# Where the tiles of a one-core fp32 model step stand in on-chip memory: tiles moved within 512 bytes

## The chip, the cores and the metric

The kernel runs on one core of a Trainium2 chip. The metric is device time in microseconds (us) for one execution of the whole program; the median of three runs of the kernel before is 1243.19 us. TensorE (PE) does the matrix products, VectorE (DVE) and ScalarE (ACT) the element-wise work, GpSimd (POOL) a few masks, SyncE (SP) issues the transfers. SBUF is the on-chip memory with 128 partitions, in which all operands of a product lie; PSUM takes the products.

## What is computed

Two model blocks in a row on 256 tokens of width 1024, all in fp32. The first has a mixer of three branches, attention over a memory of 256 rows and a squared-ReLU MLP; the second has a state-space mixer, a gated convolutional FFN, latent attention and a second such FFN. Cut to the products that the change touches:

```python
def first_block(x, mem, ...):
    h = rmsnorm(x, norm_mix_g)
    proj = h @ w_in                       # three branches and gates
    ...                                   # conv, stick-breaking attention, retention
    up = jnp.einsum('bsnw,nwd->bsnd', branches, w_branch)
    x = x + jnp.sum(gates * up, axis=2) @ w_o
    x = x + memory_attention(rmsnorm(x, norm_xa_g), rmsnorm(mem, norm_mem_g), w_xq, w_xkv, w_xo)
    h = rmsnorm(x, norm_mlp_g)
    x = x + jnp.square(jax.nn.relu(h @ w_up)) @ w_down
    return rmsnorm(x, final_g)

def second_block(h, ...):
    h = layer_norm(ALPHA * h + ssd_mixer(h, ...))
    h = layer_norm(ALPHA * h + conv_ffn(h, ffn_up[0], ..., ffn_down[0]))
    h = layer_norm(ALPHA * h + mla_attention(h, ...))
    return layer_norm(ALPHA * h + conv_ffn(h, ffn_up[1], ..., ffn_down[1]))
```

## The kernel before

All weights, some 225 MB, pass through SBUF once. They are cut into chunks of at most 2048 elements per partition. A chunk arrives in `wr` (two buffers), ACT copies it to `wh` in the fp32r format that PE multiplies, DVE writes the remainder to `wl` (four buffers each). Activations are held the same way, as pairs of a high and a low part: `ah`/`al` (the input of a stage, made by `new_act`), `brh`/`brl` (branches), `mth`/`mtl` (merged), `memTh`/`memTl`, `oTh`/`oTl`, `gTh`/`gTl`, `yTh`/`yTl`, `cTh`/`cTl`. Each product is three matmuls (`mm3`): high by high, high by low, low by high.

A matmul has two operands in SBUF. One is loaded into the array 128 columns at a time (the profile's PEld rows, LDWEIGHTS), the other streams past it (the MATMUL rows). The kernel uses both directions:

- `wstat`: weights are loaded, the activation of 256 tokens streams past them. Output names stand as `mm<-ah,wh`: the operand ahead of the comma streams.
- `xstat`: the activation is loaded, weights stream past in blocks of up to 512 columns (`mm<-wh,ah`, 512 columns).
- `wmixed`: the first three chunks of three stages, activation loaded, 256 columns of weights streaming (`mm<-wh,ah`, 256 columns).

While one matmul streams, the LDWEIGHTS of the next one runs. Streaming matmuls run in unbroken rows of some twenty to nine hundred, between which stand transposes and the small products of the attention parts.

Places in SBUF follow from the order in which pools are opened and tiles are first asked for. `dynamic_dma_scratch_size` is a reserve at the lower end of SBUF, 16 KB per partition by default. What matters in this case is the place of a tile modulo 512 bytes; all steps inside the tiles named here (the next 128 columns, the next row of 256 tokens) are multiples of 512 bytes, except in the chunks of 320 and 384 columns of one stage (`kvq`) and in one chunk of 32 columns. A helper `gap` (L938 to L940) takes room in a pool without using it; before, it is called once, in `attention` with 704 bytes.

The order of the instructions comes from a planner (`Plan`, `tick`) that works with durations by kind and size; it knows nothing of addresses. Every engine operation is recorded at line L284, the helper's `call`.

Of the kernel before, what the change touches and what calls it, by code (L numbers as in the profile page):

```python
# [6 lines left out]
F32 = mybir.dt.float32  # L7
F32R = mybir.dt.float32r
# [8 lines left out]
P = 128  # L17
D = 1024
S = 256
ALPHA = 4 ** 0.25  # L20
NG = 8
RAW, HELD = 2, 4
# [198 lines left out]
class Slots:  # L221
    def __init__(self, kern, pool, name, shape, dtype, n):
        self.kern, self.at, self.pool, self.name, self.shape, self.dtype = kern, kern.at, pool, name, shape, dtype
        self.idle = list(range(n))
        self.out, self.old, self.lent = {}, {}, {}
# [237 lines left out]
        self.sync = Lane(plan, nc.sync, "sp")  # L463


class Kern:
    def __init__(self, nc, tc, a, dbg=None):
        self.at = Plan()
        self.nc, self.tc, self.a, self.dbg = Engines(nc, self.at), tc, a, dbg
        self.plan, _ = chunk_plan()  # L470
        self.nch = len(self.plan)
        self.n_dma = self.n_prep = self.n_half = self.n_get = self.n_done = 0
        self.raw, self.held, self.subs = {}, {}, []
        self.bg = []
        self.floor = 0.0
        self.turns = {}
        self.blocked, self.table = False, None
        self.work = self.skew = 0.0
        self.sums = np.concatenate([[0.0], np.cumsum([len(ks) * max(n, P) * UNIT for _, ks, _, n, _ in self.plan])])

# [336 lines left out]

    def new_act(self):

        return (self.acts.tile([P, 8, S], F32R, tag="ah", name="ah"), self.acts.tile([P, 8, S], F32R, tag="al", name="al"), [0, 0])  # L820

    def ready(self, act, k, *taus):
        if len(act) == 3:
# [113 lines left out]

    def gap(self, pool, n):  # L938

        pool.tile([P, n // 4], F32, tag="gap", name="gap")  # L940

    def pair(self, pool, name, n):
        return tuple(pool.tile([P, n, S], F32R, tag=name + x, name=name + x) for x in "hl")
# [12 lines left out]
    def mixers(self, act):  # L956
        nc, a = self.nc, self.a
        mp, mp_close = self.open("mix")
        br = self.pair(mp, "br", 12)
        gt = Slots(self, mp, "gt", [P, 3, S], F32, 4)  # L960
        r256 = Slots(self, mp, "r256", [P, 256], F32, 6)
# [261 lines left out]
        ap_close()  # L1223
        rp, rp_close = self.open("merged", side="right")
        mt = self.pair(rp, "mt", 8)
        memT = self.pair(rp, "memT", 8)
        gm = self.bcast("mem", self.gb, "gb")
        g_mem = self.spawn(self.mem_norm(gm, memT))
        for m in range(8):
# [27 lines left out]
    def memory(self, x, mt, memT, mt_close):  # L1257
        nc, a = self.nc, self.a
        act = self.new_act()
        ga = self.bcast("xa", self.gb, "gb")  # L1260
        mp, mp_close = self.open("mem")
        oT = self.pair(mp, "oT", 8)

        kT = (mp.tile([P, 8, S], F32R, tag="kT", name="kT"), mt[1])
        qs = Slots(self, mp, "qs", [P, 2, 2, S], F32R, 2)

        pTs = [tuple(k[:, 2 * h:2 * h + 2, :] for k in kT) for h in range(4)]
# [497 lines left out]
    def attention(self, h, act):  # L1765
        nc = self.nc
        cos, sin = self.cs[:, 0], self.cs[:, 1]
        pool, close = self.open("mla")
        self.gap(pool, 704)
        cT = self.pair(pool, "cT", 5)  # L1770
        krT = pool.tile([P, S], F32, tag="krT", name="krT")
        knT = pool.tile([P, 8, S], F32, tag="knT", name="knT")
        qnT = pool.tile([P, 8, S], F32, tag="qnT", name="qnT")
        qrT = pool.tile([P, 4, S], F32, tag="qrT", name="qrT")
        v = pool.tile([P, 2, D], F32, tag="v", name="v")
        oT = self.pair(pool, "oT", 8)
        ps_ = Slots(self, pool, "p", [P, 384], F32, 3)
        pT = Slots(self, pool, "pT", [P, 384], F32, 3)
# [189 lines left out]
    def program(self):  # L1968
        nc, tc, a = self.nc, self.tc, self.a
        cs = []  # L1970

        def pool(name, bufs=1, **kw):
            cm = tc.tile_pool(name=name, bufs=bufs, **kw)
            cs.append(cm)
            return cm.__enter__()

        cp = pool("const")
        self.gb = pool("gb", 2)  # L1980
        self.dram = pool("dram", space=bass.MemoryType.DRAM)
        self.acts = pool("acts")
        cq = pool("small")
        self.tiny = pool("tiny", 4)
        self.tk = Slots(self, pool("tk"), "tk", [P, D], F32, 2)
        self.wraw, self.whi, self.wlo = pool("wraw", RAW), pool("whi", HELD), pool("wlo", HELD)
        pp = pool("ps", space=PSUM)
        self.mm = Slots(self, pp, "mm", [P, 512], F32, 4)
        self.sm = Slots(self, pp, "sm", [P, 512], F32, 4)

        x = cp.tile([P, 2, D], F32, tag="x", name="x")
        self.cst = cst = cq.tile([P, NCST], F32, tag="cst", name="cst")
        self.ones = cp.tile([P, P], F32, tag="ones", name="ones")
        nc.vector.memset(self.ones, 1.0)

        row = self.tk.get()
        o, w = ROWS["mix"]
        nc.sync.dma_start(out=row[0:1, :], in_=a["prow"][0:1, o:o + w])
        halves = [slice(512 * n, 512 * n + 512) for n in range(2)]
        for c in halves:  # L2000
            nc.sync.dma_start(out=x[:, 0, c], in_=a["x"][0:P, c])
        nc.sync.dma_start(out=cst[:, 0:P], in_=a["cst"][:, 0:P])
        self.pump(1)
        nc.sync.dma_start(out=x[:, 1, :], in_=a["x"][P:2 * P, :])
        self.pump()
        nc.sync.dma_start(out=cst[:, P:], in_=a["cst"][:, P:])
        gs = [self.mm.get() for c in halves]
        for pt, c in zip(gs, halves):
            self.mm1(pt, self.ones[0:1, :], row[0:1, c], True)
        self.tk.put(row)  # L2010
        self.pcol = cp.tile([P, NCOL], F32, tag="pcol", name="pcol")
        nc.sync.dma_start(out=self.pcol, in_=a["pcol"])
        self.ident, self.nu, self.ut = (cst[:, CST[n]:CST[n] + P] for n in ("ident", "nu", "ut"))
        self.at.one = cq.tile([1, 2], F32, tag="one", name="one")
        nc.vector.memset(self.at.one, 1.0)
        self.neg1 = cp.tile([P, P], F32, tag="neg1", name="neg1")
        nc.vector.memset(self.neg1, -1.0)
        self.mhalf = cq.tile([P, 2], F32, tag="mhalf", name="mhalf")
        nc.vector.memset(self.mhalf, -0.5)
        self.identb = cp.tile([P, P], BF16, tag="identb", name="identb")  # L2020
        nc.vector.tensor_copy(self.identb, self.ident)

        self.maskb = cp.tile([P, P], BF16, tag="maskb", name="maskb")
        nc.vector.memset(self.maskb, 0.0)
        nc.gpsimd.affine_select(out=self.maskb, in_=self.maskb, compare_op=ALU.is_ge, fill=-1e30, base=0,
                                pattern=[[-1, P]], channel_multiplier=1)

        act = self.new_act()
        self.until(self.spawn(self.rms(0, x, Halves(gs), act), first=True))

        def second():
            yield from self.rms(1, x, Halves(gs), act)
            for pt in gs:
                self.mm.put(pt)

        self.spawn(second(), first=True)
        mt, memT, mt_close = self.mixers(act)
        self.spawn(self.angles(cp))
        act, close = self.memory(x, mt, memT, mt_close)
        act = self.mlp(x, act, close)  # L2040
        act = self.ssd(x, act)
        act = self.ffn(0, x, act)
        act = self.attention(x, act)
        self.ffn(1, x, act)
        self.drain()
        assert self.n_get == self.nch
        for cm in reversed(cs):
            cm.__exit__(None, None, None)
# [21 lines left out]
```

## Time and profile before

| | |
|---|---|
| three runs | 1238.36, 1243.19, 1243.27 us |
| profiled execution, its time | 1244.83 us |
| its span from first to last instruction | 1243.1 us |
| TensorE clock granted, mean | 0.998 of full speed |
| PE busy with matmuls | 1224.7 us, 8468 matmuls |
| DVE, ACT busy | 853.9 us, 717.0 us |

Outside the span lie 1.7 us. A matmul's row in the profile lasts from its issue to its last result, so rows of successive matmuls overlap; what a matmul costs in an unbroken row is the step, the time from the start of one to the start of the next. It is read from a stretch: the length of the stretch plus the duration of one matmul (0.28 us at 256 columns, 0.39 us at 512), divided by the number of matmuls that lie in it in whole or part.

### The profile page before, as it was taken

The page shows a single profiled execution, that of the slowest core. Times are in us where ns is not written, and L with a number is a line of the kernel's source. Part 1 is how long each engine was busy: PE and PEld are TensorE (multiplying, and loading weights), DVE is VectorE, ACT ScalarE, POOL GpSimd, SP SyncE. Part 2 cuts the span into 40 slices and gives each one's busy share as a digit, 9 for nine tenths or more (in the row PEclk, how much of TensorE's full clock was granted, in tenths as well). Part 3 has the DMA queues.
Part 4 walks back from the last instruction along what each step waited for, and adds up shares of the span by engine and source line. Part 5 has one row for each costly group of instructions (what it writes and reads, how often), then busy time and mean ns, then how long its engine had stood idle before and what let it go on. Part 6 is the DMA issues. An engine that isn't in the chain of part 4 may idle for free.

```text
span 1243.1 us, 20768 instructions
## 1 busy us (share of the span) xinstructions
PE 1224.7 (99%) x8468; PEld 1120.8 (90%) x8468; DVE 853.9 (69%) x1378; ACT 717.0 (58%) x1181; POOL 53.5 (4%) x85
## 2 busy tenths in 40 slices
PE   7999999999999999999999999999999999999997
PEld 5978999989989998889999898999988888999986
DVE  5666847666746665446787797877765866888853
ACT  5666546446536554335788765666644575666641
POOL 0011000000000000000111201000000000000000
PEclk9999999999999999999999999999999999999999
DMA  7643355546544546524656555555573443455560
GB/s 254 235 167 127 146 196 219 179 156 228 176 152 159 214 172 221 201 106 166 227 190 233 193 174 194 187 172 202 184 259 118 161 181 123 172 197 182 213 256 35
DMA packets 35425, 227.71 MB, mean 183 GB/s; under 512 B 4321, under 2 KB 4993, under 8 KB 11522
## 3 DMA queue, kind: packets, MB, share of 16 engines
q1 hardware_dynamic: 35330, 226.39, 50.8%
q8 instruction: 66, 1.08, 0.4%
q14 instruction: 29, 0.24, 0.1%
HBM read 225.27 MB, written 1.10 MB: 182 GB/s over the span
## 4 chain that ended last, share of the span: by engine, by line
PE 95%; DVE 3%; DMA 1%; issue 0%; ACT 0%; POOL 0%; SPq 0%; POOLq 0%; DVEq 0%; ACTq 0%
PE mm L284 85%; PE sm L284 9%; DVE wl L284 1%; DVE x L284 1%; DMA wr<-wts 0%; DVE tk L284 0%; DMA cst<-cst 0%; POOL rs L284 0%; ACT wh L284 0%; DVE ln L284 0%; DVE al L284 0%; SPq L284 0%; POOLq L2066 0%; ACT r L284 0%; ACT ah L284 0%
## 5 line engine op out<-in xcount | busy, mean ns | idle before, releaser
L284 DVE TENSOR_TENSOR wl<-wr,wh 128x1024 fp32r<-128x1024 f32 (+3 forms) x408 | 479.4, 1198 | 173.7 <-ACT wh L284 173.0
L284 ACT CAST wh<-wr 128x1024 fp32r<-128x1024 f32 (+3 forms) x408 | 403.6, 1029 | 162.4 <-PE mm L284 87.9
L284 PE MATMUL mm<-ah,wh 128*128 128x256 f32 (+1 forms) x1496 | 421.1, 281 | 0.0
L284 PE MATMUL mm<-ah,wl 128*128 128x256 f32 (+1 forms) x1496 | 417.5, 279 | 0.0
L284 PE MATMUL mm<-al,wh 128*128 128x256 f32 (+1 forms) x1496 | 417.4, 279 | 0.0
L284 PEld LDWEIGHTS mm<-ah,wh 128*128 128x128 f32 (+1 forms) x1496 | 283.0, 189 | 1.6 <-issue 1.1
L284 PEld LDWEIGHTS mm<-ah,wl 128*128 128x128 f32 (+1 forms) x1496 | 281.0, 188 | 0.1
L284 PEld LDWEIGHTS mm<-al,wh 128*128 128x128 f32 (+1 forms) x1496 | 280.5, 188 | 0.4
L284 DVE SCALAR_TENSOR_TENSOR r<-mm,pcol,r 128x255 f32<-128x255 f32 (+2 forms) x212 | 86.9, 474 | 38.6 <-ACT r L284 38.6
L284 PE MATMUL mm<-wl,ah 128*128 128x512 f32 (+3 forms) x320 | 106.3, 338 | 3.1 <-DVE wl L284 3.0
L284 PE MATMUL mm<-wh,ah 128*128 128x512 f32 (+3 forms) x320 | 108.6, 345 | 0.0
L284 PE MATMUL mm<-wh,al 128*128 128x512 f32 (+3 forms) x320 | 105.9, 337 | 0.5 <-DVE al L284 0.5
L284 PE MATMUL mm<-wh,gTh 128*128 128x512 f32 x304 | 96.3, 391 | 0.0
L284 PE MATMUL mm<-wh,gTl 128*128 128x512 f32 x304 | 95.6, 389 | 0.0
L284 PE MATMUL mm<-wl,gTh 128*128 128x512 f32 x304 | 95.6, 390 | 0.0
L284 ACT ACTIVATE r<-mm,pcol 128x256 f32<-128x256 f32 x96 | 48.9, 560 | 46.9 <-PE mm L284 46.9
L284 PEld LDWEIGHTS mm<-wl,ah 128*128 128x128 f32 x320 | 60.3, 189 | 10.2 <-DVE wl L284 4.9
L284 PEld LDWEIGHTS mm<-wh,gTl 128*128 128x128 f32 x304 | 57.1, 188 | 11.8
L284 PEld LDWEIGHTS mm<-wl,gTh 128*128 128x128 f32 x304 | 57.1, 188 | 11.8
L284 PEld LDWEIGHTS mm<-wh,gTh 128*128 128x128 f32 x304 | 56.7, 188 | 12.0 <-issue 0.6
L284 PEld LDWEIGHTS mm<-wh,al 128*128 128x128 f32 x320 | 60.3, 189 | 7.0 <-DVE al L284 1.1
L284 PEld LDWEIGHTS mm<-wh,ah 128*128 128x128 f32 x320 | 60.3, 189 | 6.6 <-issue 0.7
(296 smaller groups left out, 1581.8 us busy)
## 6 DMA issues: line engine op xcount, KB each, us to landing
wr<-wts SPq DMA_DIRECT2D x186, 1024.0 KB, 4.9
wr<-wts SPq DMA_DIRECT2D x11, 768.0 KB, 4.3
gb<-prow SPq DMA_DIRECT2D x12, 512.0 KB, 6.8
dec<-rows SPq DMA_DIRECT2D x8, 768.0 KB, 7.5
wr<-wts SPq DMA_DIRECT2D x4, 704.0 KB, 4.2
wr<-wts SPq DMA_DIRECT2D x4, 512.0 KB, 7.0
tk<-mem SPq DMA_DIRECT2D x2, 512.0 KB, 7.9
out<-x SPq DMA_DIRECT2D x4, 256.0 KB, 2.1
```

The lines of the kernel that those rows point to most:

```text
L284: r = f(*args, **kw)
```

## The change

No instruction is added, removed or moved on any engine, and one wait is added (below). What changes is where tiles stand. The scratch reserve shrinks from 16 KB to 1 KB per partition, and its room goes to gaps: 192 bytes ahead of the weight buffers, gaps of 320 and 192 bytes in several pools, and 512 bytes more in each half of `new_act`, whose tile is entered at an offset from the list `PLACES`, one entry for each of the seven stages that ask for one.

Places modulo 512, from the addresses in the two built programs:

| tile | before | after |
|---|---|---|
| `wr`, `wh`, `wl` | 288 | 480 |
| `ah`, `al` | 480 | 288 (480 in the sixth stage, latent attention) |
| `brh`, `brl` | 288 | 288 |
| `mth`, `mtl` | 480 | 480 |
| `memTh`, `memTl` | 480 | 288 |
| `oTh`, `oTl` of the memory attention, `gT`, `yT` | 288 | 480 |
| `cTh`, `cTl` | 480 | 288 |
| `oTh`, `oTl` of the latent attention | 480 | 480 |

Call **lag** the place of the tile that streams less the place of the tile that is being loaded meanwhile, modulo 512. Then:

| products | columns streaming | lag before | lag after |
|---|---|---|---|
| `wstat` on `ah`/`al`, `memT`, `cT` | 256 | 192 | 320 |
| `wstat` on `br` | 256 | 0 | 320 |
| `wmixed` on `ah`/`al` | 256 | 320 | 192 |
| `xstat` on `ah`/`al`, `memT`, `cT` | 512 | 320 | 192 |
| `xstat` on `mt`, and on `oT` of the latent attention | 512 | 320 | 0 |
| `xstat` on `gT`, `yT`, `oT` of the memory attention | 512 | 0 | 0 |

The added wait: the mask that POOL puts on the third `dec` buffer of the state-space mixer, which waited for the buffer's transfer, now also waits for ACT, which wrote `mth` in the same place in the branch merge of the first block.

The diff, cut to its core:

```diff
+PLACES = (320, 320, 320, 320, 320, 0, 320)
...
     def new_act(self):
 
-        return (self.acts.tile([P, 8, S], F32R, tag="ah", name="ah"), self.acts.tile([P, 8, S], F32R, tag="al", name="al"), [0, 0])
+        at = PLACES[self.n_act] // 4
+        self.n_act += 1
+        h, l = (self.acts.tile([P, 8 * S + 128], F32R, tag=n, name=n)[:, at:at + 8 * S].rearrange("p (k s) -> p k s", s=S) for n in ("ah", "al"))
+        return (h, l, [0, 0])
...
     def mixers(self, act):
         mp, mp_close = self.open("mix")
+        self.gap(mp, 320)
         br = self.pair(mp, "br", 12)
...
         mt = self.pair(rp, "mt", 8)
+        self.gap(rp, 320)
         memT = self.pair(rp, "memT", 8)
+        self.gap(rp, 192)
...
         oT = self.pair(mp, "oT", 8)
+        self.gap(mp, 320)
         kT = (mp.tile([P, 8, S], F32R, tag="kT", name="kT"), mt[1])
+        self.gap(mp, 192)
...
         pool, close = self.open("mla")
-        self.gap(pool, 704)
+        self.gap(pool, 320)
         cT = self.pair(pool, "cT", 5)
...
         v = pool.tile([P, 2, D], F32, tag="v", name="v")
+        self.gap(pool, 192)
         oT = self.pair(pool, "oT", 8)
...
-        self.wraw, self.whi, self.wlo = pool("wraw", RAW), pool("whi", HELD), pool("wlo", HELD)
+        self.gap(pool("gap0"), 192)
+        self.wraw, self.whi = pool("wraw", RAW), pool("whi", HELD)
+        self.wlo = pool("wlo", HELD)
...
-    nc = bacc.Bacc("TRN2", target_bir_lowering=False, num_devices=1)
+    nc = bacc.Bacc("TRN2", target_bir_lowering=False, num_devices=1, dynamic_dma_scratch_size=1024)
```

## Rows read from the trace of the kernel before

**Rows 1.** The page, busy time: engine, us (share of span), instructions.
```profile
PE 1224.7 (99%) x8468; PEld 1120.8 (90%) x8468; DVE 853.9 (69%) x1378; ACT 717.0 (58%) x1181; POOL 53.5 (4%) x85
```

**Rows 2.** The page, chain that ended last, shares by engine.
```profile
PE 95%; DVE 3%; DMA 1%; issue 0%; ACT 0%; POOL 0%; SPq 0%; POOLq 0%; DVEq 0%; ACTq 0%
```

**Rows 3.** PE groups by form: output<-streaming,loaded, columns, count | busy us, mean ns | idle.
```profile
L284 PE MATMUL mm<-ah,wh 128*128 128x256 f32 x1488 | 418.9, 281 | 0.0
...
L284 PE MATMUL mm<-wh,gTh 128*128 128x512 f32 x304 | 96.3, 391 | 0.0
...
L284 PE MATMUL mm<-wh,ah 128*128 128x512 f32 x144 | 59.0, 410 | 0.0
...
L284 PE MATMUL mm<-wh,ah 128*128 128x256 f32 x144 | 41.0, 285 | 0.0
...
L284 PE MATMUL mm<-brh,wh 128*128 128x256 f32 x96 | 27.3, 285 | 0.0
...
L284 PE MATMUL mm<-wh,oTh 128*128 128x512 f32 x64 | 21.9, 403 | 0.0
...
L284 PE MATMUL mm<-memTh,wh 128*128 128x256 f32 x64 | 17.8, 278 | 0.0
...
L284 PE MATMUL mm<-wh,memTh 128*128 128x512 f32 x32 | 12.8, 399 | 0.0
...
L284 PE MATMUL mm<-wh,mth 128*128 128x512 f32 x32 | 10.7, 396 | 0.0
```

**Rows 4.** Timeline, PE and weight loads: start us, us, engine, line, operation.
```profile
820.06 0.28 PE L284 MATMUL mm<-ah,wl 128*128 128x256 f32 x1
820.06 0.19 PEld L284 LDWEIGHTS mm<-ah,wh 128*128 128x128 f32 x1
```

**Rows 5.** Stretches, PE alone, `wstat`: from:to, length, busy us (matmuls), clock, DMA share, GB/s.
```profile
27.00:49.00 22.00, 22.00 (x190) 1.00 0.67 242
...
139.00:182.00 43.00, 43.00 (x382) 1.00 0.52 184
...
282.00:297.00 15.00, 15.00 (x135) 1.00 0.52 192
...
399.50:470.00 70.50, 70.50 (x601) 1.00 0.54 195
...
794.50:899.40 104.90, 104.90 (x893) 1.00 0.52 181
...
1073.70:1174.70 101.00, 101.00 (x893) 1.00 0.54 188
```

**Rows 6.** Stretches, PE alone: `br` product, `gT`, `mt`, and a `z` product on `ah`.
```profile
236.00:250.00 14.00, 14.00 (x119) 1.00 0.56 198
...
470.50:556.00 85.50, 85.50 (x379) 1.00 0.49 180
...
252.00:269.00 17.00, 17.00 (x76) 1.00 0.42 155
...
641.00:650.00 9.00, 9.00 (x40) 1.00 0.32 119
```

**Rows 7.** Timeline, PE, first and last of an unbroken `wmixed` stretch, second FFN.
```profile
1058.66 0.28 PE L284 MATMUL mm<-wh,al 128*128 128x256 f32 x1
...
1064.90 0.28 PE L284 MATMUL mm<-wl,ah 128*128 128x256 f32 x1
```

**Rows 8.** Timeline, PE, first and last of an unbroken `wmixed` stretch, first FFN.
```profile
780.17 0.28 PE L284 MATMUL mm<-wh,al 128*128 128x256 f32 x1
...
786.18 0.28 PE L284 MATMUL mm<-wl,ah 128*128 128x256 f32 x1
```

**Rows 9.** The page, DMA queues: kind, packets, MB, share of 16 engines.
```profile
q1 hardware_dynamic: 35330, 226.39, 50.8%
```

**Rows 10.** Waits on PE: engine, line, waited for, us in total, times, longest.
```profile
PE sm L284 <- DVE tk L284: 3.1, 1, 3.1
PE mm L284 <- DVE wl L284: 3.0, 3, 2.0
```

More of the change, by code (lines that the diff above doesn't have):

```diff
@@ L477, in __init__ @@
         self.blocked, self.table = False, None
+        self.n_act = self.n_gap = 0
         self.work = self.skew = 0.0
@@ L938, in gap @@
     def gap(self, pool, n):
-        pool.tile([P, n // 4], F32, tag="gap", name="gap")
+        self.n_gap += 1
+        pool.tile([P, n // 4], F32, tag=f"gap{self.n_gap}", name="gap")
     def pair(self, pool, name, n):
```

## The prediction

> **What bounds the kernel now.** I read the page first. PE has matmuls in flight for 1224.7 of 1243.1 us, 99%, DVE 69% and ACT 58% [rows 1]. The chain of work that ended last lies 95% on PE [rows 2]; what PE waits for in a single group is at most 3.1 us [rows 10]. So nothing has to be taken off a wait: the time is the number of matmuls times their step, and an edit is worth what it does to the step. The groups by form come next, for the counts: of 8468 matmuls 4656 are `wstat` at 256 columns, three times the rows of 1488 and 64 [rows 3].
>
> The third view is the stretches of PE alone, and here the reader should stop. The same product, with the same operands in the same places, runs at two steps. The first FFN lies in one stretch of 104.9 us with 893 matmuls: (104.9 + 0.28) / 893 = 117.8 ns. The second FFN, same code and same addresses, takes (101.0 + 0.28) / 893 = 113.4 ns. The other long stretches fall to one or the other: 117.3 and 117.8 (from 27 and from 399.5 us), 113.3 and 113.2 (from 139 and from 282 us) [rows 5]. Nothing lies between, a stretch keeps its step from its first few matmuls on, and the clock stands at 1.00 of full speed, 2.4 GHz, in all of them. I call them **slow** and **fast**; they are 4.4 ns apart. Each stretch begins after a transpose or another small product, and its start seems to settle which it is.
>
> Where the lag is 0, as in the `br` product, the step is worse than either: (14.0 + 0.28) / 119 = 120.0 ns [rows 6]. The LDWEIGHTS of the next matmul starts in the same hundredth of a microsecond as the matmul it runs beside [rows 4], so the two read SBUF together, and my reading is that they meet in the memory and one of them pays. That reading is an inference; the three steps are rows.
>
> One rule speaks against any effect of the change. The Trainium skill (TensorE: Matmul & The Clock Gate, section "Step-by-step: what each phase is for") says that PE has two independent SBUF read ports, one for the streaming operand and one for LDWEIGHTS, and that loading the next weights takes no read bandwidth from the running matmul. By that rule the places would not matter and the sum below would be zero; the trace does not bear it out, with 120.0, 117.8 and 113.4 ns for one shape at the same clock [rows 5, 6].
>
> **The change part by part.** All is priced against the profiled execution's own 1244.83 us. That is 1.6 us above the median of the three runs, and these spread over 4.9 us. One long FFN stretch that goes from slow to fast is 893 x 4.4 ns = 3.9 us, so the spread is about what one such stretch explains, and I make no correction for it.
>
> *`wstat`, lag 192 to 320, 4656 matmuls.* Of the long stretches, 382 + 135 + 893 = 1410 of 3094 matmuls are fast [rows 5], 46%, which gives a mean step of 117.8 - 0.46 x 4.4 = 115.8 ns. What does lag 320 give at 256 columns? The kernel before has that lag already: in `wmixed` weights at place 288 stream past an activation at 480, and after the change the activation at 288 streams past weights at 480. Shape, lag and both places agree; only which of the two is the weight is exchanged. `wmixed` runs in twelve unbroken stretches (four in each of three stages). Eleven are slow: the one shown has 54 matmul starts from 1058.66 to 1064.90 us, 6.24 / 53 = 117.7 ns [rows 7]. One is fast: 54 starts from 780.17 to 786.18 us, 6.01 / 53 = 113.4 ns [rows 8]. By count of matmuls the fast share is 54 of some 410, 13%, a mean of 117.2 ns. So 4656 x (117.2 - 115.8) = **+6.8 us** (1.45 ns before rounding). Bounds: all slow, 4656 x 2.02 = +9.4 us; all fast, 4656 x -2.38 = -11.1 us. I take the value of the `wmixed` stretches since they are the nearest rows there are, at exactly this lag.
>
> *`br`, lag 0 to 320, 96 x 3 = 288 matmuls* [rows 3]: 120.0 to 117.2, **-0.8 us**; at the fast step -1.9.
>
> *`wmixed`, lag 320 to 192, 144 x 3 = 432 matmuls* [rows 3]: 117.2 to the 115.8 that `wstat` has at this lag now, **-0.6 us**; between -1.6 and +0.3.
>
> *512 columns, lag 320 to 0 (`mt`, and `oT` of the latent attention, half of its rows), 192 matmuls* [rows 3]: the `mt` stretch has a step of (17.0 + 0.39) / 76 = 228.8 ns, the `gT` stretch at lag 0 has (85.5 + 0.39) / 379 = 226.6 ns [rows 6]. 192 x -2.2 = **-0.4 us**. `kvq` goes the same way with some 90 smaller ones, which I leave out.
>
> *512 columns, lag 320 to 192 (`ah`, `memT`), (144 + 32) x 3 = 528 matmuls* [rows 3]: no row has 512 columns at lag 192. Now they stand near 229.5 ns, with a worst stretch of (9.0 + 0.39) / 40 = 234.8 [rows 6]. From below: 256 columns more cost 226.6 - 120.0 = 106.6 ns at lag 0, so the fast step would be 113.4 + 106.6 = 220.0, -5.0 us; from above, the worst stretch for all, +2.8 us. I take the difference that 256 columns show between these lags, -1.4 ns, **-0.7 us**, since it is the only row with the same two lags.
>
> *512 columns at lag 0 before and after* (`gT` and the rest): both operands move together; nothing.
>
> *The scratch reserve*: all data transfers are on one queue of the kind hardware_dynamic [rows 9], and none is issued by POOL, so I see no user of it: nothing. *The wider activation tile*: as many bytes read and written, nothing. *The added wait on POOL*: behind it stand the later masks on `dec`, and DVE's products with `dec` wait for these; but the tile in question is `mth`, which ACT finishes in the branch merge of the first block, so the wait is over before it begins: nothing, and if it were not, DVE at 69% would have to pass a delay on to PE.
>
> Sum: 6.8 - 0.8 - 0.6 - 0.4 - 0.7 = +4.3 us, 1249.1 us: **1249 us**. PE remains the bound; DVE and ACT have the same work as before.
>
> **The rivals.** *Lag 320 is fast under `wstat`* (the other side). The fast step exists at this lag: one stretch held it for 54 matmuls [rows 8]. What decides is the start of a stretch, and `wstat` stretches start after other work than those of `wmixed`, and run to 893 matmuls. If the start after the change favours fast everywhere, the sum is -11.1 - 1.9 - 0.6 - 0.4 - 0.7 = -14.7 us, **1230 us**; with the 512-column matmuls at their lower bound 1226. It is faster by over 0.5% from a fast share of some 72% on. Against it stand eleven of twelve stretches.
>
> *All slow*: +9.4 - 0.6 - 0.6 - 0.4 - 0.7 = +7.1, **1252 us**, and 1255 with the 512-column matmuls at their upper bound. This is the forecast's own upper end; with so few long stretches the share moves in steps of 3.9 us.
>
> *The lag doesn't choose the share, the starts alone do*: `wstat` keeps 46% fast, and only leaving lag 0 pays: `br` -1.2, `mt` and `oT` -0.4, **1243 us**. For it: the two steps are the same to 0.1 ns at lags 192 and 320.
>
> *The change does nothing*, because what separates fast from slow is not the place at all: **1245 us**. For it: one code at one set of places has both steps. Against it: `br` at lag 0, always at 120.0. The rule of the Trainium skill cited above (TensorE: Matmul & The Clock Gate) would give this result.
>
> **How the numbers follow.** The limit of what a measurement can tell from no change is 0.5%, 6.2 us: below 1237.0 and above 1249.4. The forecast, mostly slow stretches at lag 320, has 0.55 and lies from 1245 to 1255, so it is cut by that limit: 0.33 above, 0.22 within. Unchanged share 0.12 and no effect 0.08 fall within. The fast rival has 0.25 and lies below. Faster 0.25, same 0.42, slower 0.33. The range 1231 to 1254 leaves out the lower half of the fast rival and the worst of the all-slow end.
>
> **What would show it.** Right: the FFN stretches at steps near 117.8 ns, `br` down from 120.0, the `wmixed` stretches now of both kinds, `mt` at 226.6. Wrong: the FFN and `up` stretches at 113.4 or below (a step under 113.4 would be a third level that no row of before has); or `br` still at 120, which would mean that the place is not what counts. If the time moves and the steps don't, I have missed a wait; the chain would show it outside PE.

## The result, and the profile after

The changed kernel takes 1253.01 us (median of four runs, 1252.82 to 1253.72) against 1241.70 us for the kernel before in the same comparison (four runs, 1238.36 to 1243.27): a ratio of 1.0096, 95% interval 1.0071 to 1.0120. It is slower by about 1%, beyond the 0.5% that I had set as the limit. The forecast of 1249 itself lay just inside that limit, and I had given this side a chance of 0.33; what came is the time of my "all slow" rival (1252), 4 us above the forecast and 1 us inside the range.

The profiled execution took 1252.82 us, 8.0 us more than that of before (by the medians the change costs 11.3 us; the second profile of the kernel before, below, bears on this). The page says at once where they are not. First the busy times (engine, us, share of the span, instructions), then the shares of the chain that ended last, by engine:

```profile
PE 1234.5 (99%) x8468; PEld 1128.0 (90%) x8468; DVE 854.7 (68%) x1378; ACT 717.1 (57%) x1181; POOL 53.2 (4%) x85
```

```profile
PE 94%; DVE 3%; DMA 1%; issue 0%; POOL 0%; ACT 0%; SPq 0%; POOLq 0%; DVEq 0%; ACTq 0%
```

Beside [rows 1, 2]: PE has 9.8 us more with matmuls in flight for the same 8468 matmuls, DVE and ACT are where they were, and the chain still lies on PE. No new long wait appeared (the longest on PE is 2.4 us, 3.1 us before); matmuls became slower.

The stretches show which. Columns are from:to, length, PE busy (matmuls), clock, DMA share, GB/s; PE alone. The first six rows are `wstat` on `ah` and `memT`, then two of the `br` product, `mt`, and two stretches of 512 columns on `ah`:

```profile
26.50:48.00 21.50, 21.50 (x185) 1.00 0.68 247
139.00:184.00 45.00, 45.00 (x385) 1.00 0.49 176
283.00:298.50 15.50, 15.50 (x134) 1.00 0.53 201
402.00:472.00 70.00, 70.00 (x597) 1.00 0.54 196
798.50:903.00 104.50, 104.50 (x889) 1.00 0.51 181
1078.00:1182.50 104.50, 104.50 (x890) 1.00 0.52 182
237.00:252.00 15.00, 15.00 (x135) 1.00 0.57 211
214.20:219.60 5.40, 5.40 (x50) 1.00 0.43 142
253.00:269.50 16.50, 16.50 (x74) 1.00 0.48 172
67.50:76.50 9.00, 9.00 (x40) 1.00 0.32 117
88.50:96.50 8.00, 8.00 (x36) 1.00 0.36 131
```

With the length plus one matmul, divided by the count, the six `wstat` stretches have 117.7, 117.6, 117.8, 117.7, 117.9 and 117.7 ns. All are slow. In [rows 5] three of their counterparts were fast, the second FFN among them. `br` has left its 120.0 ns [rows 6] for 113.2 and 113.6 (113.3 in both from start to start): fast. `mt` has 228.2 by this row (227.0 from start to start), down from 228.8. And the 512-column products on `ah` went up. Here the first and the last matmul of the same stretch (start us, us, engine, line, operation), of the kernel before:

```profile
67.54 0.40 PE L284 MATMUL mm<-wl,ah 128*128 128x512 f32 x1
77.15 0.39 PE L284 MATMUL mm<-wl,ah 128*128 128x512 f32 x1
```

and of the changed kernel:

```profile
67.08 0.40 PE L284 MATMUL mm<-wl,ah 128*128 128x512 f32 x1
76.88 0.40 PE L284 MATMUL mm<-wl,ah 128*128 128x512 f32 x1
```

Both are 42 steps: 9.61 / 42 = 228.8 ns before, 9.80 / 42 = 233.3 after.

Taking every step between the starts of two successive matmuls in the trace, those aside in which something else stands between, the 8.0 us come out as follows:

| products | lag before, after | steps | mean ns before | after | us |
|---|---|---|---|---|---|
| `wstat` on `ah`, `memT`, `cT` | 192, 320 | 4672 | 115.59 (2331 fast) | 117.56 (237 fast) | +9.2 |
| 512 columns on `ah`, `memT`, `cT` | 320, 192 | 502 | 229.9 | 233.3 | +1.7 |
| `wstat` on `br` | 0, 320 | 283 | 119.8 | 114.6 (203 fast) | -1.5 |
| `wmixed` | 320, 192 | 409 | 117.2 | 116.0 (164 fast) | -0.5 |
| 512 columns on `mt`, `oT` | 320, 0 | 175 | 229.3 | 227.8 | -0.3 |
| 512 columns on `gT`, `yT`, `oT` of the memory attention | 0, 0 | 1160 | 227.1 | 227.2 | +0.1 |

They sum to +8.7; what takes back the other 0.7 us is not separated. At 512 columns, too, one lag has two steps: before, at lag 320, all unbroken rows of more than 20 matmuls on `ah` settle at 228.9 ns but two, at 233.4 (one of them is the `z` product of [rows 6]); after, at lag 192, all settle at 233.3.

### The profile page after: what moved, and what is told of

The parts are those of the page before. It is cut to its first block, busy times and chain, and to the rows that moved or that the text cites. A ratio compares the mean times of both kernels' runs of the same rounds, so it can differ in the third digit from the quotient of the medians.

```text
span 1251.1 us, 20769 instructions
## 1 busy us (share of the span) xinstructions
PE 1234.5 (99%) x8468; PEld 1128.0 (90%) x8468; DVE 854.7 (68%) x1378; ACT 717.1 (57%) x1181; POOL 53.2 (4%) x85
## 4 chain that ended last, share of the span: by engine, by line
PE 94%; DVE 3%; DMA 1%; issue 0%; POOL 0%; ACT 0%; SPq 0%; POOLq 0%; DVEq 0%; ACTq 0%
PE mm L284 85%; PE sm L284 9%; DMA wr<-wts 1%; DVE wl L284 1%; DVE x L284 1%; DVE tk L284 0%; POOL rs L284 0%; SPq L284 0%; DVE ln L284 0%; DVE al L284 0%; ACT wh L284 0%; POOLq L2082 0%; ACT r L284 0%; DVEq L2082 0%; DVE mth L284 0%
```

## The experiments

Theories at the start: *lag* (the lag decides the share of fast stretches), *place* (the place itself does), *starts* (the share comes from how stretches begin, whatever the lag), *scratch* (the smaller DMA reserve costs time).

### Lag 192 again, the rest of the change kept

```diff
-PLACES = (320, 320, 320, 320, 320, 0, 320)
+PLACES = (192, 192, 192, 192, 192, 0, 192)
```

> The changed kernel with six of the seven activations moved back to a lag of 192 behind the weights (place 160 with the weights at 480, a pair of places that neither kernel has); all else as changed. If the lag alone sets the share of fast stretches (the theory): wstat stretches of both kinds again, with some at 113.4 ns, the 512-column products on ah back from 233.3 to about 229 ns, and the time some 8 us below the changed kernel's 1253.0, at 1242 to 1248 us. If the absolute places or another part of the change do it (rival): all wstat stretches stay at 117.8 ns and the time stays within 2 us of 1253.

1238.1 us (ten runs, 1236.71 to 1239.62), against 1242.88 for the kernel before: ratio 0.9971, interval 0.9957 to 0.9985. Against the changed kernel's 1253.01, this one line is worth 14.9 us, more than I had expected (1242 to 1248 us). PE alone in the first mixer, `up`, both FFNs, then `br`, which stayed at lag 320:

```profile
139.00:182.00 43.00, 43.00 (x381) 1.00 0.51 184
402.00:468.40 66.40, 66.40 (x589) 1.00 0.57 207
793.00:893.00 100.00, 100.00 (x884) 1.00 0.53 189
1068.20:1168.70 100.50, 100.50 (x889) 1.00 0.53 189
235.00:251.00 16.00, 16.00 (x138) 1.00 0.62 223
```

113.6, 113.2, 113.4 and 113.4 ns: fast, as 3692 of 4671 `wstat` steps are. `br` has 118.0, slow. The 512-column products on `ah` are back at 229.4 ns from start to start, as expected. *Place* falls: the activation stands at 160 and the weights at 480, other places than in the kernel before, and the lag of 192 brings the fast step back. *Scratch* and the gaps are still in.

### The scratch reserve alone

```diff
-    nc = bacc.Bacc("TRN2", target_bir_lowering=False, num_devices=1)
+    nc = bacc.Bacc("TRN2", target_bir_lowering=False, num_devices=1, dynamic_dma_scratch_size=1024)
```

> The kernel before with the scratch reserve of 1 KB and nothing else; every tile moves down by 15360 bytes, which is 30 times 512, so all lags are those of before. If only the places modulo 512 count (theory): both steps as before, 1238 to 1244 us, within the spread of the kernel before. If the reserve or the absolute address counts (rival): the share of fast stretches falls, 1248 us or more.

1240.06 us (ten runs), ratio 0.9995, 0.9974 to 1.0016: nothing. All tiles moved together by 15 KB and all lags stayed. The profiled execution had 71% of the `wstat` steps fast where that of before had 50%, so the share at one lag is not fixed.

### Lags swept by stage

```diff
-PLACES = (320, 320, 320, 320, 320, 0, 320)
+PLACES = (448, 448, 384, 64, 256, 0, 128)
```

> The changed kernel with another lag in each stage: 448 for the mixers and the memory attention, 384 for up, 64 for the state-space mixer, 256 for the first FFN, 128 for the second (latent attention as changed). If the two steps of 113.4 and 117.8 ns belong to lags 192 and 320 alone, or if the lag sets how often the reads meet (theory): the steps differ by stage, with at least one lag always fast and one near 120 as at lag 0. If the starts alone decide between the two steps (rival): every stage shows 113.4 or 117.8 and each long stretch falls either way.

```diff
-PLACES = (320, 320, 320, 320, 320, 0, 320)
+PLACES = (256, 64, 448, 128, 64, 0, 384)
```

> The same with the lags dealt to other stages: 256 for the mixers, 64 for the memory attention and the first FFN, 448 for up, 128 for the state-space mixer, 384 for the second FFN. Theory: a lag keeps its step from one stage to the other, so 384 in the second FFN has the step that it has in up in the first sweep, and 64, 128, 256 and 448 likewise. Rival (the stage and its starts decide): the steps follow the stage and not the lag.

1255.6 and 1255.0 us, one run each. PE alone, in the first of the two: `up` at lag 384, first FFN at 256, second FFN at 128:

```profile
399.50:471.00 71.50, 71.50 (x598) 1.00 0.54 192
798.00:904.50 106.50, 106.50 (x890) 1.00 0.50 178
1080.00:1185.00 105.00, 105.00 (x887) 1.00 0.51 181
```

and in the second: first mixer at 256, `up` at 448, first FFN at 64, second FFN at 384:

```profile
139.00:185.00 46.00, 46.00 (x386) 1.00 0.50 174
405.00:472.50 67.50, 67.50 (x598) 1.00 0.55 198
799.50:904.00 104.50, 104.50 (x890) 1.00 0.50 181
1079.50:1184.50 105.00, 105.00 (x887) 1.00 0.51 181
```

120.0, 120.0 and 118.7 ns; 119.9, 113.3, 117.7 and 118.7 ns. Lag 256 is like lag 0, in another stage each time; 64 is slow like 320; 448 has the fast step like 192, though not always: in the first sweep the long stretch of the first mixer, at 448, ran at 113.3 and another one, of 144 matmuls, at 117.8. 128 and 384 lie at 118.7 to 120.0. Two expectations failed here: no lag is always fast, and 384 does not keep one step, with 120.0 in `up` and 118.7 in the second FFN. So a lag brings its steps, of which it can have two, from stage to stage, and the period is **256 bytes**, not the 512 in which I had counted.

### All that streams at 256 columns at lag 192

Beside the `PLACES` of the first experiment, the gaps in the pools change places, so that `br`, `memT` and `cT` are at lag 192 too (one of the places shown; the others are alike):

```diff
         mp, mp_close = self.open("mix")
-        self.gap(mp, 320)
+        self.gap(mp, 192)
         br = self.pair(mp, "br", 12)
```

> All activations that stream past weights at 256 columns (ah, br, memT, cT) and the keys of the memory attention stand at lag 192, all that weights stream past at 512 columns and that were at lag 320 before (mt, oT) at lag 0; the rest of the lag-320 products of 512 columns stays as in the kernel before. Lag theory: the br stretch falls to the fast step of 113.4 ns or stays a slow one at 117.8, memT and cT likewise, 1235 to 1238 us, 0.3 to 0.6% under the kernel before. Rival (the starts choose the share, the places only forbid lag 0): wstat falls back to about half fast, 1241 to 1244 us.

1238.45 us (nine runs, 1236.36 to 1240.39), ratio to the kernel before 0.9956, interval 0.9937 to 0.9976. First mixer, `br`, `up`, first FFN, PE alone:

```profile
138.00:183.00 45.00, 45.00 (x385) 1.00 0.50 176
235.00:250.50 15.50, 15.50 (x140) 1.00 0.60 220
400.00:467.50 67.50, 67.50 (x598) 1.00 0.56 201
792.00:892.00 100.00, 100.00 (x884) 1.00 0.53 189
```

117.6, then 112.7 (113.3 from start to start), 113.3 and 113.4. `br` gains, `cT` is fast and `memT` slow, but the first mixer, which has the same lag as in the first experiment and is the same code, fell back to slow. The time is that of the first experiment, just above the 1235 to 1238 us of the lag theory and below the 1241 of the rival: what moved is which stretches start well.

### The same lags, 32 bytes further on

The edit against the kernel of the experiment above:

```diff
-PLACES = (192, 192, 192, 192, 192, 0, 192)
+PLACES = (224, 224, 224, 224, 224, 32, 224)
...
-        self.gap(rp, 320)
+        self.gap(rp, 800)
...
-        self.gap(pool("gap0"), 192)
+        self.gap(pool("gap0"), 224)
```

> The same lags as in e5_best192, but every tile stands 32 bytes further on, so that tiles begin at a multiple of 64 bytes (weights at place 0, activations at 192) and not halfway between two. Theory of the relative place: only the lag counts, the steps stay 113.4 and 117.8 ns, and the time is that of e5_best192 within 0.3%. Rival, that the place itself counts (a row that begins halfway in a 64-byte line touches one line more than it has to): the step at 256 columns falls towards 109 ns or below, and the time by 20 us or more.

1239.16 us (ten runs), ratio 0.9973, 0.9955 to 0.9990. The first FFN, PE alone:

```profile
789.30:889.80 100.50, 100.50 (x889) 1.00 0.53 188
```

113.4 ns. No third level: the rival that rows begin halfway in something of 64 bytes falls, and for the steps only the relative place counted. 84% of the `wstat` steps were fast, against 71% in the experiment above; whether that comes from the 32 bytes is not shown.

### Lags between the multiples of 64

```diff
-PLACES = (320, 320, 320, 320, 320, 0, 320)
+PLACES = (160, 224, 224, 160, 208, 0, 176)
```

> The changed kernel with the activations of the stages at lags 160 (first mixer), 224 (memory query and first MLP), 160 (second mixer), 208 (first FFN) and 176 bytes (second FFN); the rest as in the changed kernel. If a lag of 192 is fast because it is three quarters of a period of 256 bytes, with a width of some tens of bytes, 208 and 176 are fast (113.4 ns) too, and 160 and 224 lie between 113.4 and 117.8 by share. If what counts is in units of 64 bytes, 160, 176, 208 and 224 have steps that fall to one of the neighbours (128: 118 to 120 ns, 192: 113.4, 256: 120.0). Time between 1236 and 1252 us by these.

1259.41 us, one run, the slowest of all. First mixer at 160, `up` at 224, the FFNs at 208 and 176, PE alone:

```profile
140.00:185.00 45.00, 45.00 (x386) 1.00 0.49 176
404.70:475.00 70.30, 70.30 (x597) 1.00 0.54 191
802.30:908.00 105.70, 105.70 (x889) 1.00 0.51 179
1083.30:1189.00 105.70, 105.70 (x888) 1.00 0.51 179
```

117.3, 118.2, 119.2 and 119.3 ns. Neither expectation held, nor the time (1236 to 1252 us): 208 and 176, 16 bytes beside the best lag, are not fast but slower than 160 and 224, which lie further from it, and 160, 208 and 224 fall to no neighbour at a multiple of 64. At 16 bytes beside 192 the fast step is gone; nothing nearer was run.

### The kernel before, once more

> The kernel before, unchanged, profiled in another execution. If a stretch at lag 192 is fast or slow by how it begins, and not by what it computes, some of the long stretches that were fast in the first profile are slow in this one or the other way round, each at 113.4 or 117.8 ns, and the time moves by 3 to 5 us with the share. If a stretch has its step from its place in the program, the same stretches are fast and slow as in the first profile, and the spread of the runs of before comes from elsewhere.

1240.15 us, 4.7 us less than in the first profile. Both FFNs, PE alone:

```profile
794.00:894.50 100.50, 100.50 (x889) 1.00 0.53 188
1069.30:1169.80 100.50, 100.50 (x889) 1.00 0.54 189
```

Both are at 113.4 ns; in [rows 5] the first was at 117.8, 104.9 us long. Of the 34 `wstat` stretches with more than 28 matmuls the other 33 have the step they had (`up`, for one, is slow in both). So most starts repeat and some do not, and 3.9 of the 4.7 us are this one stretch. Another that did not repeat is the `wmixed` stretch shortly ahead of it, the one that was fast in [rows 8]. Its first and last matmul, now:

```profile
779.30 0.28 PE L284 MATMUL mm<-wh,al 128*128 128x256 f32 x1
785.54 0.28 PE L284 MATMUL mm<-wl,ah 128*128 128x256 f32 x1
```

6.24 / 53 = 117.7 ns: slow, as are all twelve `wmixed` stretches here. What differed at the start of the two stretches, no run shows.

One stretch that is fast or slow also fits the spread. The runs of before taken beside the experiments, 37 in all, fall into two groups, 16 at 1238.4 to 1241.1 us and 18 at 1242.9 to 1244.5, with three at 1246.8 to 1249.4; the first profile of before, at 1244.83, goes with the second group, so a comparison with it makes the change look cheaper than the medians do. The four runs of the changed kernel, which has hardly a fast stretch to lose, lie 0.9 us apart. That each group is this one stretch is not shown, since the other runs have no trace.

### PE alone, without the model

```python
for n, m in STARTS:                       # eight: n transposes, m matmuls of 64 columns ahead
    for lag in (0, 64, 128, 192, 256, 320, 384, 448):
        run(lag, 256, 48, n, m)           # 48 matmuls: w loaded, the tile at this lag streams
...                                       # then seven lags between, and 512 columns
```

> The whole model is left out (the output is zeros): after a warm-up of 120 matmuls, PE alone runs stretches of 48 matmuls at 256 columns, loaded from one tile w, streaming from tiles s0, s64, s128 and so on up to s448 that stand at these lags from w, each lag after eight different starts (one to three transposes, or none, and up to two matmuls of 64 columns); then lags 16, 32, 48, 160, 176, 208, 224 after one start, then stretches of 24 matmuls of 512 columns at the eight lags after two starts. No transfers run and no other engine works meanwhile. If the two operands of PE meet in the memory by their lag modulo 256, the steps repeat what the kernel shows: 120.0 ns at lags 0 and 256, 117.8 mostly at 64 and 320, 113.4 or 117.8 by the start at 192 and 448, and at 512 columns 226.7 at 0 and 256 and over 228 elsewhere. Rival, that transfers or the writes of ACT and DVE take part (what meets PE's reads is other engines' traffic, and the lag only shifts where): without them every lag has one step, near 113.4 ns or below. If starts choose between fast and slow, the same lag shows both steps among its eight starts; if not, one lag has one step.

The eight stretches after two transposes and one matmul of 64 columns, in the order of the lags (start us, us from the first start to the last end):

```profile
172.09 6.00 PE L2020 MATMUL acc<-s,w 128*128 128x256 f32 x48
178.19 5.90 PE L2020 MATMUL acc<-s,w 128*128 128x256 f32 x48
184.17 5.94 PE L2020 MATMUL acc<-s,w 128*128 128x256 f32 x48
190.20 5.71 PE L2020 MATMUL acc<-s,w 128*128 128x256 f32 x48
195.99 6.00 PE L2020 MATMUL acc<-s,w 128*128 128x256 f32 x48
202.08 5.91 PE L2020 MATMUL acc<-s,w 128*128 128x256 f32 x48
208.07 5.95 PE L2020 MATMUL acc<-s,w 128*128 128x256 f32 x48
214.10 5.71 PE L2020 MATMUL acc<-s,w 128*128 128x256 f32 x48
```

The four values repeat after 256 bytes. A fast stretch is 0.2 us shorter than a slow one, 0.2 / 47 = 4.3 ns for each step. With two transposes and nothing more ahead, lag 192 is slow, and with three transposes even lag 64 is fast:

```profile
142.46 5.90 PE L2020 MATMUL acc<-s,w 128*128 128x256 f32 x48
...
225.96 5.69 PE L2020 MATMUL acc<-s,w 128*128 128x256 f32 x48
```

Over all starts, from start to start with the first four steps of a stretch left out (the first of the eight starts had its transposes put ahead of the warm-up, so that its stretches run on from one another):

| lag mod 256 | 256 columns, ns | 512 columns, ns |
|---|---|---|
| 0 | 119.8 to 120.0 | 227.2 to 227.8 |
| 64 | 117.8, and 113.3 after one start of eight | 228.7 to 229.0 |
| 128 | 118.5 to 120.0 | 231.9 to 232.7 |
| 192 | 113.3 to 113.4 after five starts of eight, 117.8 after three | 233.2 to 233.4 |

The lags between, one stretch each: 116.7 ns at 16, 116.6 at 32, 118.4 at 48, 118.6 at 160, 119.3 at 176, 119.3 at 208 and 118.4 at 224. So 192 is again fast and 16 bytes beside it not, and there are more than three levels.

The rival falls: from 125 to 460 us of this run VectorE, ScalarE and GpSimd ran nothing, the DMA moved 1 GB/s, the granted clock was 1.00, and the steps at the multiples of 64 are those of the kernel. The results go to one place at every lag, so what is left to meet is the operand that PE loads and the one that it streams; that they do is an inference. The order at 512 columns is another one: there lag 0 is best and 192 worst.

### Which starts are fast

```python
for n in (0, 1):                          # transposes ahead
    for c in range(16, 257, 16):          # columns of one further matmul ahead
        for lag in (64, 192, 320, 448):
            run(lag, 40, n, c)
```

> The model is left out again (the output is zeros). After a warm-up of 240 matmuls PE runs stretches of 40 matmuls of 256 columns, in this order: for no transpose and for one transpose ahead, for one further matmul of 16, 32 and so on to 256 columns ahead, at lags 64, 192, 320 and 448: 32 starts for each lag. What is asked is which lag gets the fast step of 113.4 ns from how many starts. Theory (a start leaves the two reads in one of a few positions to each other, and the lag decides how many of these are fast): 192 and 448 have the same starts fast, and more than half of them; 64 and 320 have the same starts fast, about one in eight; every stretch has one step, 113.4 or 117.8. Rival (the lag does not change the share; 13% against 50% in the kernel came from the starts of the stretches): all four lags have about the same number of fast starts.

The first four stretches, at lags 64, 192, 320 and 448 (columns as above):

```profile
34.34 4.96 PE L2018 MATMUL acc<-s,w 128*128 128x256 f32 x40
...
39.16 4.79 PE L2018 MATMUL acc<-s,w 128*128 128x256 f32 x40
...
43.81 4.96 PE L2018 MATMUL acc<-s,w 128*128 128x256 f32 x40
...
48.63 4.79 PE L2018 MATMUL acc<-s,w 128*128 128x256 f32 x40
```

Of 32 starts each, the fast step came after 2 at lag 64, 2 at 320, 16 at 192 and 22 at 448; every stretch had 113.3 or 117.8, to 0.2 ns, and kept it. So the lag sets the chance: 4 of 64 starts, 6%, at 64 and 320, 38 of 64, 59%, at 192 and 448. *Starts alone* falls. My expectation that 192 and 448 have the same starts fast, and 64 and 320 too, failed: 192 and 448 agree in 22 of 32, and 64 and 320 have none of their fast starts in common. Why is open. The lags always came in the same order, so the stretch ahead may be part of the start, but ahead of 192 and of 448 stood the same lag modulo 256. The kernel's shares fit: at lag 192, 50% and 69% of the `wstat` steps are fast in the two profiles of before, 71% with the small scratch alone, and 79%, 71% and 84% in the three kernels with `PLACES` for lag 192; at lag 320 it is 5%.

## Why the prediction was right, and where it was off

**What bounds the kernel.** Right. PE kept 94% of the chain and the 8 us lie in its steps. That an edit is worth what it does to the step held for every version of the model run here: the changes of the steps add up to the change of the profiled time, from the first profile of before, to within 1.6 us each time (between -9.7 and +14.3 us).

**Lag as the cause, and the loaded and the streaming operand meeting in the memory.** This was an inference from three steps; the lag now stands on the sweep and on the kernel with PE alone, where one shape runs from 113.3 to 120.0 ns at one clock by the lag and the start, with nothing else at work. Which part of the memory they meet in, no run shows. The rule that I had weighed, in the Trainium skill (TensorE: Matmul & The Clock Gate, section "Step-by-step: what each phase is for"), that the two read ports are independent and loading weights takes no bandwidth from the running matmul, does not agree with these steps; the "no effect" rival that rests on it is out.

**`wstat`, +6.8 predicted, +9.2 measured: the term that was mis-sized.** The mechanism and the rows for it were right: `wmixed`, with the roles of the tiles exchanged, did tell what lag 320 does. The size was off at the share. One fast stretch in twelve, 13% by matmuls, was a count of twelve draws, and that one stretch was slow in the second profile of the same kernel; the changed kernel had 237 of 4672 fast, 5%, and 4 of 64 starts were fast in the measurement of the starts. That is 117.56 instead of 117.2 ns, 1.6 us. The rest is the mean of before, 115.59 where I had 115.8 from the long stretches alone. It ended near its upper bound, all slow, +9.4. Of the 3.7 us from the forecast of 1249.1 to the profiled 1252.82 this term makes 2.4 us, the one of 512 columns at lag 320 to 192 another 2.4, and `br` takes back 0.7.

**`br`, -0.8 predicted, -1.5 measured.** Its bound was -1.9: two of its three stretches started fast. In the first experiment, at the same lag, all but the shortest were slow; this is luck of a few starts, and the steps of 120.0 did go.

**512 columns, lag 320 to 192, -0.7 predicted, +1.7 measured: the sign was wrong, another 2.4 us.** The step that failed is the one in which I carried the difference of 256 columns over to 512. The runs show that the order of the lags is not the same: at 512 columns 192 is the worst of the four with 233.3 ns, and no stretch of it was fast. The upper bound of +2.8, from the worst row for all, held it; the row of 234.8 ns [rows 6] (233.4 from start to start) was the nearer sign of what happens there than the difference I took.

**`wmixed`, `mt` and `oT`.** -0.6 and -0.4 predicted, -0.5 and -0.3 measured.

**Scratch, wider tiles, the wait on POOL: nothing.** The scratch by experiment. For the others, no new wait stands in the chain of the changed kernel, and the three kernels with all of `wstat` on `ah` at lag 192, which carry both, are faster than the kernel before.

**The fast rival** (1230) fell by the same count of starts. Its condition, a start that favours fast, exists at lag 320 after one in sixteen of the starts tried. A lag at which it mostly holds is 192, the lag of before.

**A better version.** Three kernels at lag 192 took 1238.1, 1238.45 and 1239.16 us with ratios to the kernel before of 0.9971, 0.9956 and 0.9973, all with intervals below 1: the change without its lag is better than both kernels by a little (0.3 to 0.4% against the kernel before, under my limit of 0.5%). `br`, `mt` and `oT` give 1.1, 1.8 and 2.0 us of it by their steps; the rest goes with the share of fast `wstat` steps, 79%, 71% and 84% against 50%, 69% and 71% in the three profiles at the lags of before. That share varies from build to build, and none of these runs shows how to choose it.

## What to carry to other kernels

Where PE is the bound, read the step of a matmul from start to start in long stretches, and look whether one shape has several; if it has, compare where the streaming tile and the tile being loaded stand to each other, modulo 256 bytes here. Choose the lag for the shape with the most matmuls and remember that the same pair of tiles used the other way round has the opposite lag: here 192 for 256 columns makes 320 for 512 columns, a good pair, and 320 makes 192, mostly slow at 256 columns and the worst of the four at 512. And before a chance is read from a few stretches, count how many independent starts stand behind it.

## What had not been expected of the hardware

The period is 256 bytes, with lags 16 bytes beside 192 as bad as 119.2 and 119.3 ns. One program takes two times for one stretch, 104.9 us in [rows 5] and 101.2 in the second profile ((100.50 + 0.28) / 889 x 893), for the same 893 matmuls, and keeps the step to the end. And the steps are exact: at 256 columns every stretch of more than 50 `wstat` matmuls at lag 192 or 320 and every one of the starts measured at lags 64, 192, 320 and 448 settles at 113.3 or 117.8 ns, to 0.2 ns, and no lag and no start gave a long stretch below 113.3 from start to start.
